# A conv-gated FFN on one core: from eight products of quarters in one pass to seven, in two passes through DRAM

## Chip, core and metric

The kernel runs on one core of one Trainium2 chip. The metric is the device time of one execution in microseconds; of several runs the median counts. All data are float32.

## What is computed

One decoder layer of width 1024 on 1024 tokens: four mixers side by side with an output projection, cross attention over 256 memory tokens, and an FFN with a causal depthwise convolution of width 3 ahead of a SiLU gate; a norm ends it. The FFN:

```python
D_MODEL, SEQ, BATCH, DEPTH, MEM_LEN, D_FF, FFN_CONV = 1024, 1024, 1, 1, 256, 2816, 3
...
def _conv_ffn(h, w_up, conv_w, w_down):
    u = _causal_dwconv(jnp.matmul(h, w_up), conv_w)
    gate, val = jnp.split(u, 2, axis=-1)
    return jnp.matmul(jax.nn.silu(gate) * val, w_down)
...
    mem_n = _rmsnorm(mem, mem_norm_w)
    h = x
    for l in range(DEPTH):
        h = h + _hybrid_mixer(_rmsnorm(h, mix_norm_w[l]), positions, ...)
        h = h + _memory_cross_attn(_rmsnorm(h, xattn_norm_w[l]), mem_n, ...)
        h = h + _conv_ffn(_rmsnorm(h, ffn_norm_w[l]), ffn_up[l], ffn_conv_w[l], ffn_down[l])
    return _rmsnorm(h, final_norm_w)
```

## The kernel before

**Matmuls in three parts.** Every large product is made of float32r parts: an operand is split into a high part (ScalarE casts it, line 865) and a low part (VectorE subtracts the high part from the source, line 103 by way of `split`), and three matmuls form hi x hi, lo x hi and hi x lo (`mm3`, lines 900, 901 and 903). Line 103 is the helper `tt`, through which every tensor_tensor of VectorE and GpSimd goes, so groups are told apart by their tiles.

**Stages.** The mixers' last part runs into the output projection (`wout`), which ends at 728 us, queries and scores follow, then the second output projection (`wo`), whose products `evac` adds to the residual `t`, stores to `hT` in DRAM, scales by the norm's gain and splits into `hh` and `hl`. `Sums` collects the squares; `rstd` makes the norm's factor `rbc` from them for each half of the tokens.

**FFN.** `ffn` runs one loop over f = 0 to 21, 128 hidden columns each. `hidden(f)` calls `conv_tile` for the gate (tiles `ug`, `zg`) and the value (`uv`, `zv`): a weight tile of 128 columns over all 1024 inputs (one load of 512 KB, `raw`, split into `whi` and `wlo`) is multiplied with both halves of the tokens, 8 x 3 matmuls of 512 columns each; VectorE multiplies the result by `rbc` (tokens' norm), ScalarE and VectorE form the convolution (lines 1519 and 1521), ScalarE the SiLU, VectorE the gate product and its low part (`hidh`, `hidl`). Two f behind, `down_proj` multiplies two f of hidden columns with two row blocks of `ffn_down` (`wdh`, `wdl`; the last call has four) and adds each result into `out`, eight blocks of 128 tokens. The last call also squares, scales by the final gain (GpSimd, `wbc`), forms the norm's factor in small steps on VectorE (`ss`, lines 136 to 142), scales and stores.

**Order.** A scheduler places the instructions on each engine when the program is built; each engine then runs its own list in order and waits on semaphores. All DMAs are issued by SyncE, in order. Tiles come from pools with a fixed number of buffers; a new tile waits until the old one in its place has been read.

## Time and profile before

| | us |
|---|---|
| median of 3 runs (range) | 1688.33 (1683.96 to 1690.45) |
| profiled execution, its own time | 1686.75 |
| its span, first to last instruction | 1685.0 |
| of it from the first FFN matmul to the end | 744.6 |

The profile names a group of instructions by engine, line, operation and tiles (`ug<-hh,whi`: written from read), with its count, busy time and mean duration. TensorE's matmuls overlap in the pipeline, so a mean of 390 ns is longer than the distance between two of them. An idle time is put down to the instruction that ended it. Of a window the profile gives each engine's busy time in it and the granted clock of TensorE as a share of the full one.

### The profile page before, as it was taken

The page shows a single profiled execution, that of the slowest core. Times are in us where ns is not written, and L with a number is a line of the kernel's source. Part 1 is how long each engine was busy: PE and PEld are TensorE (multiplying, and loading weights), DVE is VectorE, ACT ScalarE, POOL GpSimd, SP SyncE. Part 2 cuts the span into 40 slices and gives each one's busy share as a digit, 9 for nine tenths or more (in the row PEclk, how much of TensorE's full clock was granted, in tenths as well). Part 3 has the DMA queues.
Part 4 walks back from the last instruction along what each step waited for, and adds up shares of the span by engine and source line. Part 5 has one row for each costly group of instructions (what it writes and reads, how often), then busy time and mean ns, then how long its engine had stood idle before and what let it go on. Part 6 is the DMA issues. An engine that isn't in the chain of part 4 may idle for free.

```text
span 1685.0 us, 26532 instructions
## 1 busy us (share of the span) xinstructions
PE 1635.3 (97%) x10501; PEld 1366.0 (81%) x10501; DVE 1033.4 (61%) x1702; ACT 624.6 (37%) x1212; POOL 279.5 (17%) x330
## 2 busy tenths in 40 slices
PE   6999998999999999999999999999999999999996
PEld 6887786888877897788888888888888888888885
DVE  6765596536676545654565466557557556565577
ACT  6543633233474234343454352313213213123133
POOL 3401214323326414210012100000000000000013
PEclk8999999999999999999999999999999999999998
DMA  8743447663384344652245432102102112111012
GB/s 278 227 153 111 131 125 169 171 177 120 105 245 136 107 139 139 189 171 76 82 125 175 147 124 63 55 21 76 50 26 75 44 32 63 38 51 63 26 43 95
DMA packets 238551, 187.17 MB, mean 111 GB/s; under 512 B 34284, under 2 KB 210779, under 8 KB 238427
## 3 DMA queue, kind: packets, MB, share of 16 engines
q1 hardware_dynamic: 238427, 185.47, 36.3%
q8 instruction: 83, 1.36, 0.3%
q14 instruction: 41, 0.34, 0.1%
HBM read 138.75 MB, written 46.68 MB: 110 GB/s over the span
## 4 chain that ended last, share of the span: by engine, by line
PE 78%; DVE 9%; DMA 5%; issue 2%; ACT 2%; SPq 1%; POOL 1%; ACTq 0%; DVEq 0%; POOLq 0%
PE ug L903 5%; PE ug L900 5%; PE ug L901 5%; PE uv L901 5%; PE uv L903 5%; PE uv L900 5%; PE dn L900 4%; PE dn L903 4%; PE dn L901 4%; DVE wlo L103 2%; PE q L900 2%; PE wo L903 2%; PE wo L900 2%; PE q L901 2%; PE wo L901 2%
## 5 line engine op out<-in xcount | busy, mean ns | idle before, releaser
L103 DVE TENSOR_TENSOR wlo<-raw,whi 128x1024 fp32r<-128x1024 f32 (+1 forms) x150 | 196.2, 1308 | 108.6 <-ACT whi L865 101.3
L865 ACT CAST whi<-raw 128x1024 fp32r<-128x1024 f32 (+1 forms) x150 | 157.6, 1051 | 191.2 <-PE q L901 39.2
L103 DVE TENSOR_TENSOR out<-dn,out 128x512 f32<-128x512 f32 x160 | 109.2, 688 | 66.0 <-PE dn L903 65.4
L903 PE MATMUL ug<-hh,wlo 128*128 128x512 f32 x352 | 137.7, 392 | 0.0
L901 PE MATMUL ug<-hl,whi 128*128 128x512 f32 x352 | 137.3, 390 | 0.0
L900 PE MATMUL ug<-hh,whi 128*128 128x512 f32 x352 | 137.2, 390 | 0.0
L901 PE MATMUL uv<-hl,whi 128*128 128x512 f32 x352 | 137.1, 390 | 0.0
L903 PE MATMUL uv<-hh,wlo 128*128 128x512 f32 x352 | 137.1, 389 | 0.0
L900 PE MATMUL uv<-hh,whi 128*128 128x512 f32 x352 | 137.0, 389 | 0.0
L901 PE MATMUL dn<-wdl,hidh 128*128 128x512 f32 x320 | 124.7, 390 | 0.0
L900 PE MATMUL dn<-wdh,hidh 128*128 128x512 f32 x320 | 124.7, 390 | 0.0
L903 PE MATMUL dn<-wdh,hidl 128*128 128x512 f32 x320 | 121.9, 390 | 0.0
L1519 ACT ACTIVATE ug<-zg,taps 128x512 f32<-128x512 f32 x44 | 31.7, 722 | 201.1 <-DVE zg L103 196.5
L103 DVE TENSOR_TENSOR zg<-ug,rbc 128x512 f32<-128x512 f32 x44 | 30.2, 689 | 87.9 <-PE ug L903 87.9
L900 PEld LDWEIGHTS ug<-hh,whi 128*128 128x128 f32 x352 | 66.1, 188 | 14.0 <-issue 0.2
L901 PEld LDWEIGHTS ug<-hl,whi 128*128 128x128 f32 x352 | 66.1, 188 | 14.0
L903 PEld LDWEIGHTS ug<-hh,wlo 128*128 128x128 f32 x352 | 66.1, 188 | 13.9 <-issue 0.2
L900 PEld LDWEIGHTS uv<-hh,whi 128*128 128x128 f32 x352 | 66.1, 188 | 13.7
L903 PEld LDWEIGHTS uv<-hh,wlo 128*128 128x128 f32 x352 | 66.1, 188 | 13.6
L901 PEld LDWEIGHTS uv<-hl,whi 128*128 128x128 f32 x352 | 66.1, 188 | 13.6
L1521 DVE SCALAR_TENSOR_TENSOR ug<-zg,taps,ug 128x512 f32<-128x512 f32 x88 | 65.7, 750 | 13.1 <-ACT ug L1519 10.5
L865 ACT CAST hidh<-ug 128x512 fp32r<-128x512 f32 x44 | 27.3, 621 | 124.8 <-DVE ug L103 124.8
(463 smaller groups left out, 4166.1 us busy)
## 6 DMA issues: line engine op xcount, KB each, us to landing
raw<-in_ffn_up SPq DMA_DIRECT2D x44, 512.0 KB
raw<-in_w_in SPq DMA_DIRECT2D x26, 512.0 KB
raw<-in_ffn_down SPq DMA_DIRECT2D x22, 512.0 KB
raw<-in_w_out SPq DMA_DIRECT2D x16, 512.0 KB
hT<-t SPq DMA_DIRECT2D x32, 256.0 KB
raw<-in_xattn_wq SPq DMA_DIRECT2D x16, 512.0 KB
raw<-vod SPq DMA_DIRECT2D x16, 512.0 KB
raw<-in_xattn_wk SPq DMA_DIRECT2D x8, 512.0 KB
```

The costliest lines, as they stand in the source:

```text
L103: e.tensor_tensor(out=out, in0=a, in1=b, op=op)
L865: nc.scalar.copy(hi, src)
L900: nc.tensor.matmul(o, lhsT=w.hi, rhs=x.hi, start=first, stop=False)
L901: nc.tensor.matmul(o, lhsT=w.hi, rhs=x.lo, start=False, stop=False)
L903: nc.tensor.matmul(o, lhsT=w.lo, rhs=x.hi, start=False, stop=last)
L1519: S_.mul(u, z[:, 2 + o:2 + o + 512], taps[:, 2, n:n + 1])
L1521: V.scalar_tensor_tensor(u, z[:, j + o:j + o + 512], taps[:, j, n:n + 1], u, op0=ALU.mult, op1=ALU.add)
```

## The change

The FFN becomes two passes. Both products are cut into quarters (two halves of the tokens or hidden columns, two halves of what is summed over), and each 2 x 2 product of quarters is formed of seven products by the Winograd form of Strassen's algorithm, with sums and differences of quarters ahead of it and sums of the products behind it.

- *Up pass* (`ffn_up`): the four result quarters are gate and value columns of f, by the two halves of the tokens. The activations are now normed before they are split: the first half's blocks `x` (`early`) are made while the second half of `wo` runs, and the five combined blocks `t1`, `t2`, `t3`, `n4`, `b22` by `rest` after it. Of the weights, GpSimd forms four sums per f (`s1` to `s4`), and seven operands of 128x512 are split (`ws`) in place of two of 128x1024. Two of the seven products per f need only `early` and run three f ahead (`lead`). VectorE adds the products up (`u2`, `u3`, `zv1`, `zv0`, `zg1`) from PSUM; the convolution stays. The gate's weights are loaded twice.
- *Between*: instead of being split and used at once, the gated hidden columns go to DRAM as the seven left operands of the down product (`hd`, three as they are and four sums by GpSimd for each pair of f, `left_sums`), and GpSimd forms four differences of quarters of `ffn_down` for each pair (`right_sums`, `dd`).
- *Down pass* (`ffn_down_`): seven products, each over 11 pairs of operands that are loaded and split (left by VectorE, right by GpSimd), into four PSUM banks; sums into `out` by VectorE and GpSimd. The norm of token blocks 4 to 7 is finished ahead of the last product.
- Constants of the mixers move to a pool that is closed after them; the tiles of the two passes lie where older pools were.

```diff
-        h = cross_attention(K, ap_, h1p, hp2, h, r, xattn_wq[0], kd, vod, hT, col("ffn"), rbc)
+        prep = cross_attention(K, ap_, h1p, hp2, h, r, xattn_wq[0], kd, vod, hT, col("ffn"))
+        att2.close()
+        wts2.close()
+        down_ops = ffn_up(K, ap_, h1p, prep, ffn_up_w[0], ffn_conv_w, ffn_down[0])
         att.close()
-        ffn(K, ctx, h, rbc, ffn_up[0], ffn_conv_w, ffn_down[0], hT[1], final_norm_w, out)
+        hps.close()
+        ffn_down_(K, down_ops, ffn_down[0], hT[1], final_norm_w, out)
...
+        if hf == 0:
+            for k in range(NK):
...
+                t = wide(ap_, "x0")
+                nc.sync.dma_start(out=t, in_=hT[1][k][:, cs])
+                V.scalar_tensor_tensor(t, t, gain[:, k:k + 1], rb, op0=ALU.mult, op1=ALU.mult)
+                nc.sync.dma_start(out=xd[k], in_=t)
+                d = early[-1][:, k % 4]
+                split(K, t, d.hi, d.lo)
+    def rest(blocks):
+        t1, t2, t3, n4, b22 = blocks
...
+        for k in range(4):
+            x0 = wide(ap_, "x0")
+            nc.sync.dma_start(out=x0, in_=xd[k])
+            lo, hi = late[k], late[4 + k]
+            for j, t in ((k, lo), (4 + k, hi)):
+                V.scalar_tensor_tensor(t, t, gain[:, j:j + 1], rb, op0=ALU.mult, op1=ALU.mult)
+            tt(V, x0, lo, x0, ALU.subtract)
+            split(K, x0, t1[:, k].hi, t1[:, k].lo)
+            tt(V, x0, hi, x0, ALU.subtract)
+            split(K, x0, t2[:, k].hi, t2[:, k].lo)
...
+def product(K, acc, w, x, begin):
+    for k in range(4):
...
+        K.nc.tensor.matmul(acc, lhsT=a.hi, rhs=b.hi, start=begin and k == 0, stop=False, **o)
+        K.nc.tensor.matmul(acc, lhsT=a.hi, rhs=b.lo, start=False, stop=False, **o)
+        K.nc.tensor.matmul(acc, lhsT=a.lo, rhs=b.hi, start=False, stop=k == 3, **o)
+LEAD = 3
...
+                  {"raw": 3, "ws": 7, "s": 2, "dc": 4})
...
+        def lead(f):
+            g = columns(f)
+            acc = mx(K, "p12")
+            product(K, acc, parts(g[:, 0:4]), early[0], True)
+            u = wide(ap_, "u2")
+            S_.copy(u, acc)
+            product(K, acc, parts(g[:, 4:8]), early[1], False)
...
+            S_.copy(z[:, 2:], acc)
+            return u, z
...
+        def hidden(f, u2, zg0):
+            g, v = columns(f), columns(22 + f)
+            ws = {}
+            def total(name, a, b, op):
+                t = wp.tile([P, 4, P], F32, tag="s", name=name)
+                tt(G, t, a, b, op)
+                ws[name] = parts(t)
+                return t
+            s1 = total("s1", v[:, 0:4], v[:, 4:8], ALU.add)
+            s2 = total("s2", s1, g[:, 0:4], ALU.subtract)
+            acc = mx(K, "p6")
+            product(K, acc, ws["s2"], t2, True)
+            tt(V, u2, u2, acc, ALU.add)
+            total("s3", g[:, 0:4], v[:, 0:4], ALU.subtract)
...
+            product(K, c, ws["s3"], t3, True)
+            tt(V, u3, u2, c, ALU.add)
...
+            product(K, d, ws["s1"], t1, True)
+            tt(V, zv1[:, 2:], u3, d, ALU.add)
+            total("s4", g[:, 4:8], s2, ALU.subtract)
+            product(K, c, parts(v[:, 4:8]), n4, False)
+            tt(V, zv0[:, 2:], u2, c, ALU.add)
+            product(K, d, ws["s4"], b22, False)
+            tt(V, zg1[:, 2:], u2, d, ALU.add)
...
+            for zg, zv in ((zg0, zv0), (zg1, zv1)):
+                a, b = conv(zg, f, "ug"), conv(zv, 22 + f, "uv")
+                S_.activation(a, a, AF.Silu)
+                tt(V, a, a, b, ALU.mult)
...
+        def left_sums(j, e, o):
...
+            out(0, e[0]), out(1, o[0]), out(3, o[1])
+            total(6, e[0], e[1], ALU.subtract)
+            s1 = total(4, e[1], o[1], ALU.add)
+            s2 = total(5, s1, e[0], ALU.subtract)
+            total(2, o[0], s2, ALU.subtract)
+        def right_sums(j):
...
+            for i, (d, a, b) in enumerate(((b11, b12, b11), (b12, b22, b12), (b22, b22, b11), (b21, b21, b22))):
+                tt(G, d, a, b, ALU.subtract)
+                nc.sync.dma_start(out=dd[(0, 2, 1, 3)[i]][j], in_=d)
+        ahead = [lead(f) for f in range(LEAD)]
...
+        rest((t1, t2, t3, n4, b22))
+        for f in range(22):
+            res = hidden(f, *ahead.pop(0))
+            if f + LEAD < 22:
+                ahead.append(lead(f + LEAD))
...
+def ffn_down_(K, ops, down, hT, final_w, out):
...
+                  {"u": 8, "rh": 4, "hs": 13, "rd": 4, "ds": 13, "res": 2, "ss": 3})
...
+        def operand(src, raw, tag, eng):
+            r = bp.tile([P, 512], F32, tag=raw, name=raw)
+            nc.sync.dma_start(out=r, in_=src)
+            t = bp.tile([P, 2, 512], F32R, tag=tag, name=tag)
+            S_.copy(t[:, 0], r)
+            tt(eng, t[:, 1], r, t[:, 0].bitcast(F32), ALU.subtract)
...
+        def prod(i, accs, begin):
+            for j in range(11):
+                h, d = operand(hd[i][j], "rh", "hs", V), operand(right(i, j), "rd", "ds", G)
+                for a, ts in zip(accs, tiles):
+                    add(a, h, d, ts, begin and j == 0, j == 10)
```

What the scheduler makes of it, at three places. VectorE, one f in the middle of the loop before (`hidden` with its two weight tiles and a split of `ffn_down`):

```order
L103 TENSOR_TENSOR zg_13699<-ug_13707,rbc0_63 128x512
L1521 SCALAR_TENSOR_TENSOR ug_13733<-zg_13699,taps_9710,ug_13733 128x512 x2
L103 TENSOR_TENSOR zg_13699<-ug_13737,rbc1_64 128x512
L103 TENSOR_TENSOR wlo_13852<-raw_13849,whi_13851 128x1024
L1521 SCALAR_TENSOR_TENSOR ug_13763<-zg_13699,taps_9710,ug_13763 128x512 x2
L103 TENSOR_TENSOR zv_13767<-uv_13775,rbc0_63 128x512
L103 TENSOR_TENSOR wdl_13998<-raw_13995,wdh_13997 128x1024
```

VectorE now, a stretch of the 22 operations of one f (`ws` the low parts of weights, `u2<-u2,p6` and `u3<-u2,p74` sums that read PSUM):

```order
L1612 SCALAR_TENSOR_TENSOR ug_11991<-zg0_11519,taps_9736,ug_11991 128x512
L101 TENSOR_TENSOR ws_12189<-raw_12186,ws_12189 128x512
L1612 SCALAR_TENSOR_TENSOR uv_11995<-zv0_11950,taps_9736,uv_11995 128x512
L1612 SCALAR_TENSOR_TENSOR ug_12001<-zg1_11952,taps_9736,ug_12001 128x512
L101 TENSOR_TENSOR u2_11678<-u2_11678,p6_12078 128x512
L1612 SCALAR_TENSOR_TENSOR uv_12005<-zv1_11951,taps_9736,uv_12005 128x512
L101 TENSOR_TENSOR ws_12206<-raw_12186,ws_12206 128x512
L101 TENSOR_TENSOR ug_11991<-ug_11991,uv_11995 128x512
L1612 SCALAR_TENSOR_TENSOR ug_12001<-zg1_11952,taps_9736,ug_12001 128x512
L101 TENSOR_TENSOR u3_12110<-u2_11678,p74_12097 128x512
```

Splits of half the width and sums from PSUM now stand among the conv steps. GpSimd before, from the last sum of squares ahead of the FFN into the loop:

```order
L103 TENSOR_TENSOR acc1_9411<-acc1_9411,sq_9690 128x512
L1512 MEMSET zg_9851 128x2
L1512 MEMSET zv_9919 128x2
L1512 MEMSET zg_9999 128x2
L1512 MEMSET zv_10067 128x2
```

GpSimd now, in the up pass (`ls` left sums, `rs` right sums):

```order
L101 TENSOR_TENSOR ls_11710<-ug_11640,ls_11707 128x512
L101 TENSOR_TENSOR rs_11873<-rs_11875,rs_11873 128x512
L1604 MEMSET zg0_11870 128x2
L101 TENSOR_TENSOR rs_11875<-rs_11877,rs_11875 128x512
L101 TENSOR_TENSOR rs_11877<-rs_11877,rs_11873 128x512
L101 TENSOR_TENSOR rs_11879<-rs_11879,rs_11877 128x512
L101 TENSOR_TENSOR s1_12068<-raw_12066 128x512
L101 TENSOR_TENSOR s2_12073<-s1_12068,raw_12064 128x512
L1638 MEMSET zv0_11950 128x2
L101 TENSOR_TENSOR s3_12092<-raw_12064,raw_12066 128x512
L101 TENSOR_TENSOR ls_12052<-ug_11815,ug_11825 128x512
L101 TENSOR_TENSOR s4_12130<-raw_12064,s2_12073 128x512
```

The additions are new on this engine; weight sums stand between left sums, which read VectorE's results. SyncE before, where `ffn_down` is first loaded (a load stands among others and has its own buffer):

```order
L1542 DMA raw_10443<-in_ffn_down 128x1024
L1503 DMA res_9835<-hT1_7338 128x512
L1503 DMA res_9843<-hT1_7338 128x512
L1542 DMA raw_10449<-in_ffn_down 128x1024
L892 DMA raw_10593<-in_ffn_up 128x8x128
```

SyncE now, at the turn from the up to the down pass:

```order
L1660 DMA hd3_9751<-ug_13680 128x512
L1660 DMA hd4_9752<-ls_13696 128x512
L1660 DMA hd5_9753<-ls_13699 128x512
L1660 DMA hd2_9750<-ls_13702 128x512
L1714 DMA wbc_13717<-in_final_norm_w 128x1024
L1722 DMA rh_13723<-hd0_9748 128x512
L1722 DMA rd_13728<-in_ffn_down 128x512
L1722 DMA rh_13745<-hd0_9748 128x512
```

The down pass's loads (`rh`, `rd`) stand behind the last stores of left sums.

## Rows read from the trace of the kernel before

**Rows 1.** The page's busy table: busy us, share of the span, instructions.
```profile
span 1685.0 us, 26532 instructions
...
PE 1635.3 (97%) x10501; PEld 1366.0 (81%) x10501; DVE 1033.4 (61%) x1702; ACT 624.6 (37%) x1212; POOL 279.5 (17%) x330
```

**Rows 2.** Windows by stage: us, busy by engine (instructions), PEclk, DMA share, GB/s.
```profile
940.00:1030.00 90.00, 90.00 (x428) 74.23 (x427) 53.27 (x72) 42.64 (x61) 2.99 (x11) 1.00 0.37 120
1030.00:1130.00 100.00, 100.00 (x442) 82.65 (x441) 59.53 (x82) 20.19 (x28) 0.50 (x5) 1.00 0.13 41
1630.00:1685.00 55.00, 39.60 (x171) 31.71 (x169) 40.89 (x129) 16.98 (x41) 20.62 (x16) 0.91 0.21 77
```

**Rows 3.** Tile `ug` (ns min/median/max, first and last start); the timeline's last matmul.
```profile
L900 PE MATMUL ug<-hh,whi x352: 387/389/510, 940.4 to 1613.3; 128*128 128x512 f32 x176
...
1669.20 0.40 PE L903 MATMUL dn<-whi,hidl 128*128 128x512 f32 x1
```

**Rows 4.** Timeline of VectorE where it has a queue: start, us, operation.
```profile
980.10 0.68 DVE L103 TENSOR_TENSOR ug<-ug,uv 128x512 f32<-128x512 f32 x1
980.70 0.74 DVE L1521 SCALAR_TENSOR_TENSOR ug<-zg,taps,ug 128x512 f32<-128x512 f32 x1
981.37 0.68 DVE L103 TENSOR_TENSOR hidl<-ug,hidh 128x512 fp32r<-128x512 f32 x1
981.97 1.41 DVE L1521 SCALAR_TENSOR_TENSOR ug<-zg,taps,ug 128x512 f32<-128x512 f32 x2
```

**Rows 5.** Groups by line: count, busy us, mean ns, idle before.
```profile
L103 POOL TENSOR_TENSOR out<-out,wbc 128x512 f32<-128x512 f32 x16 | 20.6, 1294 | 49.8 <-ACT sq L1565 49.8
...
L865 ACT CAST hidh<-ug 128x512 fp32r<-128x512 f32 x44 | 27.3, 621 | 124.8 <-DVE ug L103 124.8
```

**Rows 6.** Timelines of VectorE and GpSimd where both work at once.
```profile
1649.40 0.16 DVE L141 SCALAR_TENSOR_TENSOR ss<-ss 128x1 f32<-128x1 f32 x1
1649.42 1.30 POOL L103 TENSOR_TENSOR out<-out,wbc 128x512 f32<-128x512 f32 x1 [1.71 <-ACT sq L1565]
1649.60 1.15 DVE L142 SCALAR_TENSOR_TENSOR ss<-ss 128x1 f32<-128x1 f32 x1
...
614.39 0.68 DVE L103 TENSOR_TENSOR xl<-ot,xh 128x512 fp32r<-128x512 f32 x1
614.60 1.04 POOL L103 TENSOR_TENSOR oev<-oev,rs 128x512 f32<-128x512 f32 x1 [4.68 <-DVE zev L103]
615.00 1.20 DVE L103 TENSOR_TENSOR zev<-zev,oev 128x512 f32<-128x512 f32 x1
...
863.45 0.75 DVE L869 SCALAR_TENSOR_TENSOR hl<-t,cols,hh 128x512 fp32r<-128x512 f32 x1
863.58 1.77 POOL L103 TENSOR_TENSOR acc<-acc,sq 128x512 f32<-128x512 f32 x1 [5.88 <-ACT sq L1084]
```

**Rows 7.** Timeline: the second half's norm, first activation and last operation.
```profile
951.45 0.69 ACT L129 ACTIVATE rbc<-rps,consts 128x512 f32<-128x512 f32 x1 [5.55 <-PE rps L124]
...
957.13 0.69 DVE L103 TENSOR_TENSOR rbc<-rbc,nt 128x512 f32<-128x512 f32 x1
```

**Rows 8.** Timeline: a load of 256 KB is issued, and the operation that waits for it.
```profile
923.28 0.43 SPq L1473 DMA_DIRECT2D t<-hT  x1
...
927.34 0.69 DVE L103 TENSOR_TENSOR t<-wo,t 128x512 f32<-128x512 f32 x1 [0.65 <-DMA t<-hT]
```

**Rows 9.** Windows near the start, columns as in rows 2.
```profile
12.00:16.00 4.00, 1.54 (x5) 1.25 (x6) 4.00 (x7) 1.93 (x3) 1.52 (x1) 0.58 1.01 401
...
20.00:24.00 4.00, 4.00 (x37) 4.00 (x36) 2.98 (x7) 4.00 (x8) 2.62 (x2) 1.00 0.89 274
```

**Rows 10.** Timeline of the tail: the last row block's addition.
```profile
1676.16 0.68 DVE L103 TENSOR_TENSOR out<-dn,out 128x512 f32<-128x512 f32 x1
```

## What the change is expected to do

> **What bounds the kernel now.** I read the busy table first: TensorE is busy for 97% of the span, VectorE for 61%, GpSimd for 17% [rows 1]. That invites the thought that fewer matmuls mean less time. The table by stage then says where: from 940.4 us, where the first matmul of the FFN starts [rows 3], to the end, 744.6 of 1685.0 us are FFN. In its middle TensorE never stops, at full granted clock: 442 matmuls in 100.00 us, one each 0.226 us, while VectorE works 59.5 us of 100 and GpSimd 0.5 [rows 2]. There TensorE sets the pace, and the other two have room. At the very end it is otherwise: the last matmul starts at 1669.20 [rows 3], the last row block is added at 1676.16 [rows 10], and VectorE is busy 40.9 us of the last 55 [rows 2].
>
> **What is removed.** Up is 44 x 2 x 8 x 3 = 2112 matmuls of 512 columns before, down 22 x 8 x 2 x 3 = 1056. Seven products in place of eight give 22 x 7 x 12 = 1848 and 7 x 11 x 4 x 3 = 924. That is 396 fewer, at 0.226 us: **-89.6 us**, if TensorE still sets the pace. One step of 128 hidden columns (one f) costs TensorE 96 x 0.226 = 21.7 us before and 84 x 0.226 = 19.0 us after. Everything else is a question of whether the others keep up with 19.0.
>
> **What is added in the up pass.** The order of VectorE and GpSimd shows the pattern. Per f VectorE has 22 operations of 128x512: seven splits of weights, five sums that read one operand from PSUM, eight conv steps, two gate products. Where VectorE has a queue in the trace, a tensor_tensor follows the next after 0.60 us and a conv step after 0.67 [rows 4], so it needs 14 x 0.60 + 8 x 0.67 = 13.8 us. Alone that fits under 19.0. ScalarE has seven casts of about 0.62 [rows 5] and seven copies and activations, under 10 us, and is not late. GpSimd, which had only memsets here, gets eight additions per f: four sums of weights, and four for the operands of the down pass (right sums on even f, left sums on odd). A GpSimd operation of this shape and with two inputs takes 1.29 us [rows 5]: 10.4 us per f.
>
> These two cannot be put side by side. In the tail of the trace a VectorE operation on one column takes 0.16 us, and 1.15 when a GpSimd multiply has just started; at 614.60 a GpSimd operation of 1.04 us lets the operation that reads PSUM pass at its usual 0.68, and the next, with both inputs in SBUF, takes 1.20 in place of 0.68. At 863.58 it is GpSimd that waits: its addition lasts 1.77, until 1.15 us after VectorE's step has ended [rows 6]. So an addition on GpSimd and an operation of VectorE with two SBUF inputs take turns. The Trainium skill has this as a rule, in "SBUF — State Buffer", section "Who interferes with whom": a VectorE instruction with two SBUF inputs contends with a GpSimd instruction that reads SBUF, and whoever is second waits for the whole of the other; with one SBUF input it does not contend. Taken literally, with the row's 1.29 held whole, an addition would cost 0.22 us more than below, 1.8 us per f, and the sum would be some 38 us higher; the rows show the shorter hold, and I go by them.
>
> Of the 22 operations 17 have two SBUF inputs and five read PSUM. An addition that comes before one of the 17 costs VectorE about 1.05 us (0.16 to 1.15, and the waits of the others alike); before one of the five some 0.5, since that one passes meanwhile. Mean: (17 x 1.05 + 5 x 0.5) / 22 = 0.93, times eight = 7.4 us. VectorE then needs 13.8 + 7.4 = 21.2 us per f, and I add 0.2 for a place where it waits for GpSimd itself (a weight sum stands behind a left sum in GpSimd's queue): **21.4 us per f, which is above TensorE's 19.0**. Bounds: below, TensorE's own 19.0 (all additions fall into waits of VectorE); above, 13.8 + 10.4, all of GpSimd's time added, 24.2. I take 21.4 because in a full queue the additions have no waits to fall into. So VectorE sets the pace of the up pass.
>
> **The path, step by step.** (1) Second half of the output projection: between two of its weight splits VectorE gets ten operations, 6 us, where a weight tile lasts 24 x 0.226 = 5.4; TensorE waits some 2 us: the projection ends at 942.4. (2) The first weights of the up pass lie where the old weight pool lies, and their loads stand behind it. A load of half the size lands 4.06 us after its issue [rows 8]; six casts follow, then the last norm: from its first activation at 951.45 to its last operation at 957.13, 0.69 long, the trace has 6.4 us [rows 7]. VectorE starts on the activations' operands at about 956.4, 14 us later. Meanwhile TensorE waits some 6 us and then has six lead products, 16.5 us. (3) The five combined blocks: 41 operations of VectorE, 25 us, and 16 of GpSimd's additions among them, 16 x 0.93 = 15: 996. (4) From there to the end of the up pass VectorE has 473 operations in its order, 21.5 times 22: 21.5 x 21.4 = 460: 1456. (5) The turn to the down pass: in SyncE's order the first loads of the down pass stand behind the last store of the up pass, and that behind GpSimd's last left sum. Three sums of 1.29, four issues of about 0.4, a landing of 3.5, two casts, one split of 1.29: 11 us in which TensorE has nothing. After its first long wait the trace granted it 0.58 of the clock on average in 12 to 16 us, much of that at the lower of its two levels (1.2 and 2.4 GHz), and the full clock from 20 [rows 9]; the same here costs about 3 us more: 1470. (6) Down pass: 924 x 0.226 = 209, and 12 for the transposes of the residual and what lay between the matmuls of the FFN before (1669.6 - 940.4 - 3168 x 0.226): 1691. A pair of operands costs VectorE 0.6 and GpSimd 1.29 against TensorE's 12 x 0.226 = 2.7, with 13 buffers ahead: hidden; GpSimd's 28 other operations, 36 us, fit too (77 x 1.29 + 36 = 135 of 209). If they did not, up to 15 us would come on top. (7) Tail: one addition and one multiply per row block are left where there were two each; from the last block's addition to the end it is 8.8 us [rows 1, 10], and I take 12 from the last matmul on, where 15.4 were: 1703 to 1704.
>
> The span of the profiled execution is 1685.0, its time 1686.75, so 1.75 lies around it; the median of the runs shown is 1.6 us above that time. **1704 + 1.75, about 1706 us**, 1.0% slower than the median. The 90 us that TensorE is spared are spent by VectorE (21.4 - 19.0 over 21.5 steps, 52 us), by the start (some 25), and by the turn between the passes (some 30 with the last conv).
>
> **Rivals.** A, faster: GpSimd's additions fall into gaps in which VectorE waits for ScalarE or TensorE anyway. For it speaks that VectorE's order was laid out with such waits; against it that a queue of 13.8 us of work with eight interruptions leaves few. If all are hidden, TensorE sets the pace: from 949, 22 x 19.0 = 418 and a wait of 10 for the first blocks, 17 for the last conv and the turn, 3, 221, 12, 1.75: 1632. It decides from where a step falls below 21.4 - (1706 - 1688)/21.5 = 20.5 us: there the kernel is no longer slower. Half hidden is about 1660. B, slower still: the queues lock step. Three weight buffers per f, GpSimd's and SyncE's queues in fixed order, and a load of the next weights that stands behind a store of a left sum: one wait of a sum, a cast and a split, 2.6 us per f, gives 24 us and 1762. For it speaks that these queues mix work of both kinds; against it that a load has some 12 us of VectorE's order to land in. That the change does not do what it says is no rival: the order has the fewer matmuls.
>
> **How the numbers follow.** The forecast (a step between 20.3 and 22.8 us) has 0.55, with 1680 to 1737 as its own range; A 0.27, with 1632 to 1680; B 0.18, with 1737 to 1790. A tenth is left out on either side: 1645 to 1758. 0.5%, about 8.4 us, is what a measurement of this kernel can tell from no change: below 1680 lies A with 0.26; 1680 to 1697 takes 0.17, the lower part of the forecast; above it 0.57.
>
> **What would show it.** Right: a step of the up pass of 21 to 22 us, TensorE idle some 2 us in each, its waits put down to VectorE's or ScalarE's split of weights; VectorE's splits and conv steps at a mean well above 0.69 and 0.75 while the sums that read PSUM stay at 0.69; a gap of TensorE of 15 to 20 us before the down pass, and a down pass without gaps. Wrong: TensorE above 97% busy in the up pass (A), or VectorE idle for several us of each step, waiting for GpSimd or a load (B).

## The result: 1.2% slower, with the parts at other sizes

The changed kernel took a median of 1706.46 us (1703.65 to 1708.32), the kernel before, run beside it, 1686.14 (1681.43 to 1690.45): a ratio of 1.012, 95% interval 1.0085 to 1.0155. The profiled execution took 1704.68, of which the span is 1702.5. Of the four runs of `v1_right_early`, in the table further down, one took 2548.85 us at a granted clock of 0.555 where the others have 0.973 to 0.980, and the time given there is the median of these three. The busy table, against [rows 1]:

```profile
span 1702.5 us, 27454 instructions
...
PE 1579.4 (93%) x10105; PEld 1301.4 (76%) x10105; DVE 1149.9 (68%) x1745; ACT 736.4 (43%) x1514; POOL 694.1 (41%) x605
```

TensorE has 396 fewer matmuls and is busy 56 us less, but the span is 17.5 us longer. Where it idles stands in the windows by stage (columns as in [rows 2]):

```profile
943.00:960.00 17.00, 15.91 (x57) 11.71 (x58) 12.54 (x14) 10.00 (x15) 8.80 (x8) 0.81 0.80 249
960.00:995.00 35.00, 20.30 (x61) 13.45 (x59) 31.16 (x33) 14.70 (x27) 20.53 (x15) 0.76 0.39 120
...
1100.00:1400.00 300.00, 282.31 (x1172) 224.46 (x1171) 268.55 (x308) 122.27 (x236) 170.60 (x141) 0.97 0.51 165
...
1450.00:1470.00 20.00, 4.35 (x10) 3.47 (x11) 8.48 (x11) 5.91 (x10) 7.97 (x6) 0.50 0.69 249
```

In [rows 2] TensorE was busy 100.00 of 100 us in the middle of the FFN; here it is 282.31 of 300, VectorE is at 268.55 where it had 59.5 of 100, and GpSimd at 170.60. TensorE's large holes are the start of the FFN and the turn between the passes. Its timeline (start, duration, idle time before it in brackets) has them, a small one in the down pass, and the last matmul:

```profile
944.09 2.07 PE L129 MATMUL rps<-acc,ones 128*128 128x512 f32 x2 [10.59 <-POOL acc L101]
...
1465.65 2.07 PE L1730 MATMUL dn<-ds,hs 128*128 128x512 f32 x4 [21.91 <-ACT ds L1724]
...
1503.03 2.08 PE L1730 MATMUL dn<-ds,hs 128*128 128x512 f32 x4 [3.52 <-ACT ds L1724]
...
1693.36 0.39 PE L1732 MATMUL dn<-ds,hs 128*128 128x512 f32 x1
```

The length of a step of the up pass is read from one small operation that each step has once, ScalarE's copy of two columns into `zv`; these are the copies of f = 3 and f = 19:

```profile
1072.21 0.19 ACT L1642 COPY zv<-zv 128x2 f32<-128x2 f32 x1
...
1418.02 0.19 ACT L1642 COPY zv<-zv 128x2 f32<-128x2 f32 x1
```

Sixteen steps in 345.81 us are **21.6 us each**; VectorE is busy 268.55/300 of that, 19.3 us, and idles 2.3. All steps below are read in this way.

How GpSimd and VectorE meet is seen in the timeline of VectorE, and under it GpSimd's of the same moment:

```profile
1056.79 0.74 DVE L1612 SCALAR_TENSOR_TENSOR uv<-zv,taps,uv 128x512 f32<-128x512 f32 x1
1057.46 1.78 DVE L101 TENSOR_TENSOR ws<-raw,ws 128x512 fp32r<-128x512 f32 x1
1059.16 1.78 DVE L101 TENSOR_TENSOR ug<-ug,uv 128x512 f32<-128x512 f32 x1
1060.86 0.67 DVE L101 TENSOR_TENSOR u<-u,p 128x512 f32<-128x512 f32 x1
...
1057.07 3.32 POOL L101 TENSOR_TENSOR rs<-rs 128x512 f32<-128x512 f32 x2 [0.74 <-POOL rs L101]
1060.35 1.72 POOL L101 TENSOR_TENSOR s<-raw 128x512 f32<-128x512 f32 x1
```

Two operations of VectorE with both inputs in SBUF last 1.78 in place of 0.68, the next, which reads PSUM (`p`), its usual 0.67; GpSimd's own last 1.7 in place of 1.29. Over the stretch from 1100 to 1400 us the groups by line (count, busy us, mean ns, idle time before) say the same: splits, conv steps and gate products at about 1.0 us, sums from PSUM at 0.675.

```profile
L101 DVE TENSOR_TENSOR ws<-s,ws 128x512 fp32r<-128x512 f32 x56 | 59.9, 1078 | 30.2 <-ACT ws L870 30.2
L1612 DVE SCALAR_TENSOR_TENSOR uv<-zv,taps,uv 128x512 f32<-128x512 f32 x56 | 55.3, 987 | 0.0
...
L101 DVE TENSOR_TENSOR ug<-ug,uv 128x512 f32<-128x512 f32 x28 | 31.9, 1139 | 0.7
L101 DVE TENSOR_TENSOR zv<-u,p 128x512 f32<-128x512 f32 x28 | 18.9, 675 | 0.5 <-PE p L1554 0.5
```

These means mix operations that were held with operations that were not: of the conv steps `uv` the median has 743 ns and the longest 1781. The waits of the same stretch (us in total, times, longest) form a chain. TensorE waits for VectorE's sums, VectorE for ScalarE's casts of weight sums, and ScalarE for GpSimd, which makes these sums:

```profile
ACT ws L870 <- POOL s L101: 104.0, 27, 9.6
...
DVE ws L101 <- ACT ws L870: 30.2, 15, 3.1
...
PE p L1552 <- DVE u L101: 16.1, 6, 3.5
```

### The profile page after: what moved, and what is told of

Same layout as the page of the kernel before. It is cut to its first block, busy times and chain, and to the rows that moved or that the text cites. A ratio compares the mean times of both kernels' runs of the same rounds, so it can differ in the third digit from the quotient of the medians.

```text
span 1702.5 us, 27454 instructions
## 1 busy us (share of the span) xinstructions
PE 1579.4 (93%) x10105; PEld 1301.4 (76%) x10105; DVE 1149.9 (68%) x1745; ACT 736.4 (43%) x1514; POOL 694.1 (41%) x605
## 3 DMA queue, kind: packets, MB, share of 16 engines
q1 hardware_dynamic: 307531, 275.34, 51.6%
q8 instruction: 79, 1.29, 0.3%
## 5 line engine op out<-in xcount | busy, mean ns | idle before, releaser
L101 DVE TENSOR_TENSOR wlo<-raw,whi 128x1024 fp32r<-128x1024 f32 (+2 forms) x104 | 133.5, 1283 | 87.0 <-ACT whi L870 80.4
L870 ACT CAST whi<-raw 128x1024 fp32r<-128x1024 f32 (+2 forms) x104 | 109.1, 1050 | 155.2 <-PE q L906 42.0
L101 DVE TENSOR_TENSOR hs<-rh,hs 128x512 fp32r<-128x512 f32 x77 | 92.5, 1222 | 99.4 <-ACT hs L1724 97.1
L1730 PE MATMUL dn<-ds,hs 128*128 128x512 f32 x308 | 115.9, 399 | 25.4 <-ACT ds L1724 25.4
L101 POOL TENSOR_TENSOR ds<-rd,ds 128x512 fp32r<-128x512 f32 x77 | 114.6, 1507 | 57.8 <-ACT ds L1724 56.7
L1731 PE MATMUL dn<-ds,hs 128*128 128x512 f32 x308 | 122.2, 397 | 0.0
L1732 PE MATMUL dn<-ds,hs 128*128 128x512 f32 x308 | 121.5, 394 | 0.0
L101 DVE TENSOR_TENSOR ws<-s,ws 128x512 fp32r<-128x512 f32 x88 | 89.5, 1028 | 45.2 <-ACT ws L870 45.1
L1553 PE MATMUL p<-t,ws 128*128 128x512 f32 x264 | 107.6, 407 | 4.8 <-DVE t L101 4.7
L1552 PE MATMUL p<-t,ws 128*128 128x512 f32 x264 | 107.0, 407 | 5.2 <-ACT ws L870 2.9
L1554 PE MATMUL p<-t,ws 128*128 128x512 f32 x264 | 107.0, 407 | 3.3 <-DVE ws L101 3.3
L101 POOL TENSOR_TENSOR rs<-rs 128x512 f32<-128x512 f32 x44 | 71.2, 1618 | 48.4 <-DMA rs<-in_ffn_down 25.8
L1730 PEld LDWEIGHTS dn<-ds,hs 128*128 128x128 f32 x308 | 58.7, 193 | 38.1 <-ACT ds L1724 26.1
L1612 DVE SCALAR_TENSOR_TENSOR uv<-zv,taps,uv 128x512 f32<-128x512 f32 x88 | 87.4, 997 | 0.0
L1552 PE MATMUL p<-x,ws 128*128 128x512 f32 x176 | 69.4, 404 | 8.0 <-ACT u L1601 8.0
L1553 PE MATMUL p<-x,ws 128*128 128x512 f32 x176 | 70.5, 401 | 0.0
L1554 PE MATMUL p<-x,ws 128*128 128x512 f32 x176 | 70.4, 401 | 0.0
```

The costliest lines, as they stand in the source:

```text
L101: e.tensor_tensor(out=out, in0=a, in1=b, op=op)
L870: nc.scalar.copy(hi, src)
L1552: K.nc.tensor.matmul(acc, lhsT=a.hi, rhs=b.hi, start=begin and k == 0, stop=False, **o)
L1553: K.nc.tensor.matmul(acc, lhsT=a.hi, rhs=b.lo, start=False, stop=False, **o)
L1554: K.nc.tensor.matmul(acc, lhsT=a.lo, rhs=b.hi, start=False, stop=k == 3, **o)
L1612: V.scalar_tensor_tensor(u, z[:, j:j + 512], taps[:, j, n:n + 1], u, op0=ALU.mult, op1=ALU.add)
```

## The experiments

Two theories. *Turns*: GpSimd's additions and VectorE's operations with two SBUF inputs take turns, and this sets the step. *Queue*: the step is set by a loop through GpSimd's and SyncE's queues (buffer free, load, sum, cast, split). All kernels were timed beside the kernel before; the ratios are to it. The order of each engine's list is laid out anew for every kernel, so an edit also moves some instructions: compared by operation and tile in the traces, of VectorE's 1745 operations in the changed kernel 1725 keep their order in `e10_stores_gpsimd`, some 1690 in `e1_no_sums` and `e6_more_s`, 1620 in `e8_no_turns`, 1600 in `e5_conv_psum` and 1590 in `e9_psum_and_s`.

| kernel | us | ratio (95% interval) | step, us | VectorE busy in it |
|---|---|---|---|---|
| the change | 1706.46 | 1.012 (1.0085 to 1.0155) | 21.6 | 19.3 |
| e1_no_sums | 1657.1 | 0.9823 (0.9804 to 0.9842) | 19.6 | 14.4 |
| e2_all_vector | 1679.86 | 0.9955 (0.9938 to 0.9971) | 20.0 | 18.9 |
| e3_weights_vector | 1694.82 | 1.0032 (1.0018 to 1.0046) | 20.8 | 19.8 |
| e4_leftright_vector | 1694.36 | 1.0050 (1.0034 to 1.0067) | 20.7 | 19.6 |
| v1_right_early | 1675.95 | 0.9922 (0.9897 to 0.9948) | 19.4 | 17.6 |
| e5_conv_psum | 1719.43 | 1.0176 (1.0151 to 1.0201) | 21.7 | 16.0 |
| e6_more_s | 1701.38 | 1.0063 (1.0038 to 1.0089) | 20.8 | 20.6 |
| e8_no_turns | 1655.84 | 0.9798 (0.9782 to 0.9814) | 19.3 | 14.2 |
| e9_psum_and_s | 1740.02 | 1.0284 (1.0263 to 1.0305) | 22.4 | 17.5 |
| v2_right_in_q | 1675.22 | 0.9919 (0.9893 to 0.9945) | 19.4 | 17.6 |
| e10_stores_gpsimd | 1723.86 | 1.0200 (1.0183 to 1.0217) | 22.3 | 20.5 |

**What all additions cost.**

```diff
-                t = wp.tile([P, 4, P], F32, tag="s", name=name)
-                tt(G, t, a, b, op)
+                t = a
...
-                t = wp.tile([P, 512], F32, tag="dc", name="ls")
-                tt(G, t, a, b, op)
+                t = a
...
-                tt(G, d, a, b, ALU.subtract)
```

The three places are the weight sums, the left sums and the right sums.

> Left out: all eight additions of GpSimd in each step of the up pass; a weight sum or an operand of the down pass is then simply its first summand, with the same splits, products and stores, so TensorE's work is that of the changed kernel. In the changed kernel a step of the up pass lasts 21.6 us (two steps 43.0) where its 84 matmuls at 0.226 us are 19.0. Theory (GpSimd's additions and VectorE's operations with two SBUF inputs take turns, and that sets the step): VectorE needs 13.8 us of a step, TensorE sets the pace again, the step falls to 19.0 to 19.5, and the time by 21 x 2.3 = 48, to about 1657; splits and conv steps fall from a mean of 1.0 to 0.69 and 0.75. Rival (what limits is the distance from a weight's load to its split, or the loads and stores themselves, which stay): under a third of that, 1690 or more. The turn to the down pass (21.9 us of TensorE) shrinks by the three last sums, 4 us, under both.

1657.1, as expected. TensorE is busy without a break, and a step is the 19.6 us of its 84 matmuls, 0.233 each:

```profile
1100.00:1400.00 300.00, 300.00 (x1291) 242.59 (x1289) 220.12 (x341) 135.37 (x259) 2.81 (x28) 1.00 0.38 120
```

So the additions on GpSimd cost the kernel 49 us. It takes away turns and queue alike; the next ones tell these apart.

**The same additions on VectorE**, all or half of them (`tt(G` to `tt(V` in the lines above).

> All eight additions of a step are on VectorE, none on GpSimd. Theory (turns between GpSimd and VectorE set the step): VectorE then needs 13.8 + 8 x 0.60 = 18.6 us, less than the 21.2 that it needs with the turns, though it does more; TensorE's 19.0 sets the pace, with some waits since the two are so near: 19.0 to 20.3 a step, 1652 to 1680. Rival (VectorE is late because it has too much in its queue, not because of GpSimd): 18.6 + the 2.2 us a step that VectorE waits now = 20.8 or more, 1690 and above.

> The four sums of weights of a step are on VectorE, the four for the down pass stay on GpSimd. Theory (turns, 0.93 us of VectorE for each addition on GpSimd): 13.8 + 4 x 0.60 + 4 x 0.93 = 19.9, a step of 20.1, 1.5 x 21.5 = 32 us less: about 1674. Rival (not the turns but the way of a weight sum through GpSimd's queue, a cast and a split makes TensorE wait): all that can be had is had here, 19.2 a step, about 1655, and nothing in the kernel with the other four moved.

> The four additions of a step for the operands of the down pass are on VectorE, the four sums of weights stay on GpSimd. Theory (turns): the same as with the weights moved, 13.8 + 2.4 + 3.7 = 19.9 for VectorE, about 1674. Rival (the way of a weight sum through GpSimd's queue is what counts): the weight sums have the same way as before, less the places where they stand behind a left or right sum: 0 to 10 us less, 1696 to 1706.

With eight more operations in its list VectorE is busy 18.9 us a step, less than the 19.3 that it had without them, and the kernel is 26 us faster: that speaks for turns, and the time lies at the upper end of what was expected.

```profile
1100.00:1400.00 300.00, 290.44 (x1247) 233.35 (x1245) 282.51 (x453) 135.62 (x255) 2.88 (x29) 1.00 0.55 175
```

But of the 1.6 us that a step lost, only some 0.5 is VectorE's busy time. The other 1.1 is time in which it idled: 2.3 us of a step in the changed kernel, 1.1 here. So GpSimd's additions cost VectorE waits as well as busy time.

Four of eight moved give 12 us, whichever four, where 32 were expected, and VectorE's busy time even grows by 0.3 to 0.5, so all of this gain is in the waits. With the left and right sums moved the 12 us are nearer to the rival's 0 to 10 than to the theory. That it doesn't matter which four speaks against the queue of the weight sums as the sole cause; that it is 12 says that the price of 0.93 was too high.

**The price by itself**, in the kernel before, where nobody waits for the result.

```diff
     def hidden(f):
+        for _ in range(8):
+            tt(G, spare, wbc[:, 0:512], wbc[:, 512:1024], ALU.add)
```

> The kernel before, with eight additions of 128x512 on GpSimd added for each f, two inputs in SBUF, for whose result nobody waits: the price of one addition by itself. VectorE is busy 19.7 of the 33.1 us of an f there (up and down together). Theory (turns): VectorE's busy time in the FFN grows by 0.6 to 0.93 for each addition, 5 to 7.4 us per f, its splits and conv steps grow, its operations that read PSUM do not, and as 27 us is still under 33.1 TensorE and the time stay as they are, 1680 to 1695. Rival (what made the changed kernel's VectorE slow was something else, as its own operands or the loads): VectorE's busy time as before, within 0.5 us per f.

The additions did not spread; they ran in bunches of up to 22, and the last of the 176 ended at 1262 us. In the window 1030 to 1130 GpSimd is busy 92.88 us, and VectorE needs 79.84 for 68 operations where [rows 2] has 59.53 for 82:

```profile
1030.00:1130.00 100.00, 90.69 (x384) 73.57 (x383) 79.84 (x68) 23.83 (x33) 92.88 (x65) 0.95 0.15 43
```

The groups from 1030 to 1530 us have conv steps at 1.16 and leave the products that read PSUM (`zg<-ug,rbc`) untouched; the kernel before has 750 and 690 ns there. More than half of that stretch has no additions: from 1030 to 1130 alone the conv steps `ug` are at 1.68.

```profile
L1521 DVE SCALAR_TENSOR_TENSOR ug<-zg,taps,ug 128x512 f32<-128x512 f32 x56 | 64.8, 1156 | 8.0 <-ACT ug L1519 5.5 <-POOL spare L103 0.9
...
L103 DVE TENSOR_TENSOR zg<-ug,rbc 128x512 f32<-128x512 f32 x28 | 19.3, 689 | 50.8 <-PE ug L903 50.8
```

The kind of effect is as expected, the price is lower. Over the whole FFN VectorE is busy 547.05 us, and 463.13 in the kernel before: 83.9 us for 176 additions, 0.48 each, where 0.6 to 0.93 were expected. First the kernel with the additions, then the kernel before:

```profile
940.00:1739.00 799.00, 742.99 (x3244) 608.69 (x3243) 547.05 (x698) 210.46 (x305) 300.41 (x238) 0.97 0.18 55
```

```profile
940.00:1685.00 745.00, 729.60 (x3240) 601.88 (x3238) 463.13 (x697) 211.99 (x304) 27.13 (x62) 0.99 0.18 58
```

The time was a miss: 50 us more (1740.36 beside 1690.35) in place of none, since in a bunch VectorE does fall behind TensorE, which waited 27.0 us for `zv`. A share of VectorE over a whole f hides that.

**Turns without queue, queue without turns.** First one more buffer for the weight sums (`"s": 2` to `"s": 3`), then the conv's running sums in PSUM:

```diff
-            u = wide(ap_, name)
-            S_.mul(u, z[:, 2:514], taps[:, 2, n:n + 1])
-            for j in (1, 0):
-                V.scalar_tensor_tensor(u, z[:, j:j + 512], taps[:, j, n:n + 1], u, op0=ALU.mult, op1=ALU.add)
+            u, ps = wide(ap_, name), mx(K, "cv")
+            S_.mul(ps, z[:, 2:514], taps[:, 2, n:n + 1])
+            for d, j in ((ps, 1), (u, 0)):
+                V.scalar_tensor_tensor(d, z[:, j:j + 512], taps[:, j, n:n + 1], ps, op0=ALU.mult, op1=ALU.add)
```

> One change of a number: three buffers in place of two for the sums of weights, so that GpSimd waits less often for VectorE to have split the last one. In the changed kernel VectorE idles 2.3 us of a step of 21.6. Theory (turns): the busy 19.3 us stay, of the 2.3 up to half goes, 0 to 1.1 us a step, 1682 to 1706. Rival (the queues lock step through the few buffers): 1.5 us a step or more, 1673 or less.

> The running sums of the conv lie in PSUM until their last step writes them to SBUF, so that the eight conv steps per step of the up pass read one operand from SBUF and one from PSUM; nothing else changes, all eight additions stay on GpSimd. VectorE's busy time per step is 19.3 us in the changed kernel and 14.4 without GpSimd's additions, so these cost 4.9 us of it. Theory (only an operation with two SBUF inputs takes turns with GpSimd): 8 of 17 such operations are out of it, 4.9 x 8/17 = 2.3 us less, a step of 19.6 to 20.3, 1666 to 1682; conv steps at 0.74 throughout, splits still above 0.9. Rival (GpSimd slows whatever VectorE does, or the step comes from the wait for the weight sums): conv steps still near 1.0, 1700 or more. Not told apart by it: if the four shared PSUM buffers make TensorE wait for the conv, that shows as waits of TensorE for VectorE's conv.

With the third buffer the step is 20.8, and VectorE is busy 296.43 of 300 us: there it has no waits left, and its busy time with the turns in it is the limit. The 0.8 us that the step lost are put down to the queue with two buffers, as little else moved. They are less than the 2.3 us that VectorE idled, since its busy time rose from 19.3 to 20.6 when the waits went. The kernel's time fell by 5 us only (the profiled executions by 8.6), not least because the steps began later: the copy of f = 3 stands at 1075.73, not at 1072.21.

```profile
1100.00:1400.00 300.00, 286.42 (x1215) 228.37 (x1213) 296.43 (x316) 127.15 (x245) 193.35 (x150) 0.99 0.56 174
```

With the conv in PSUM its steps are at 0.74 to 0.75, as the theory of turns has it. Of the splits those of weight sums stay long, 0.99 where they had 1.08, but those of loaded weights fell to 0.78. And the time, 1719.43, is in the rival's range, not the theory's: the step did not shorten. What VectorE saved, 3.3 us, came back as waits, for ScalarE's casts (51.6 us where the changed kernel has 30.2) and for TensorE (15.0 at `zv` where it has 0.5). ScalarE itself now waited 46.9 us for weight buffers that TensorE held, 5.7 in the changed kernel. So this run neither shows nor refutes that the turns set the step: another limit took their place. The four PSUM buffers, shared by more tiles, are the likely one, but no run tests it.

```profile
L101 DVE TENSOR_TENSOR ws<-s,ws 128x512 fp32r<-128x512 f32 x56 | 55.4, 989 | 51.6 <-ACT ws L870 51.2
...
L1612 DVE SCALAR_TENSOR_TENSOR cv<-zv,taps,cv 128x512 f32<-128x512 f32 x28 | 21.0, 751 | 6.9 <-ACT cv L1610 6.4
...
L101 DVE TENSOR_TENSOR zv<-u,p 128x512 f32<-128x512 f32 x28 | 19.3, 689 | 15.0 <-PE p L1554 14.5
```

**The test that settles it.** An addition is replaced by one of two columns and two memsets, which occupy GpSimd and read nothing:

```diff
+def fill(G, t, a, b, op):
+    tt(G, t[:, 0:2], a[:, 0:2], b[:, 0:2], op)
+    for _ in range(2):
+        G.memset(t[:, 2:512], 0.0)
...
-                tt(G, t, a, b, op)
+                fill(G, t, a, b, op)
```

> Each of GpSimd's eight additions of a step becomes an addition of two columns and two memsets of the rest, which read nothing: the same tiles, the same waits and the same place in GpSimd's queue, about 1.2 us each, but hardly any reading of SBUF. The sums' values are left out by it. With the conv's running sums in PSUM VectorE was busy only 16.0 us of a step, and the step stayed at 21.7, so the turns cannot be all. Theory A (turns alone set the step): 19.6 to 19.9 us a step, as with no additions at all, 1657 to 1666. Theory B (the loop through GpSimd's queue alone: buffer free, sum, cast, split): 21.3 or more, 1698 to 1706. Theory C (both: VectorE's busy time with the turns is one limit, near 20.8, and the loop, whose parts the turns lengthen, is the other): 19.9 to 21.2, 1666 to 1696.

1655.84, as with no additions at all and just under the range of theory A. The window, VectorE's tiles (min/median/max ns) and one of GpSimd's groups:

```profile
1100.00:1400.00 300.00, 297.37 (x1283) 240.49 (x1281) 220.15 (x344) 137.15 (x260) 164.37 (x399) 1.00 0.56 177
```

```profile
L101 DVE TENSOR_TENSOR ws<-s,ws x60: 677/684/694, 1108.2 to 1381.8; 128x512 fp32r<-128x512 f32 x60
...
L1618 DVE SCALAR_TENSOR_TENSOR uv<-zv,taps,uv x65: 737/744/750, 1100.6 to 1399.1; 128x512 f32<-128x512 f32 x65
```

```profile
L1405 POOL MEMSET s<- 128x510 f32 x118 | 59.5, 521 | 0.4
```

GpSimd is busy 10.6 us a step, as eight additions of 1.29 alone would make it (12.3 in the changed kernel, where VectorE holds up the additions too), yet no operation of VectorE is held: the longest split has 694 ns, the longest conv step 753. And the queue is no better off; GpSimd's waits in the same stretch (us in total, times, longest), first here, then in the changed kernel:

```profile
POOL s L101 <- DMA raw<-in_ffn_up: 63.7, 13, 8.3
...
POOL s L101 <- DVE ws L101: 41.5, 20, 6.6
```

```profile
POOL s L101 <- DVE ws L101: 40.0, 21, 3.2
POOL s L101 <- DMA raw<-in_ffn_up: 39.9, 7, 6.7
```

The waits are there, and cost nothing as long as the parts of the loop are not lengthened. Of the three ranges only A's fits: without the reading, TensorE sets the pace. So GpSimd's reading beside VectorE is the cause of the long step. The run takes the holding off both engines at once; it does not tell how much of the lost time is VectorE's own longer operations and how much is GpSimd's sums coming later. For that there is only the third buffer's 0.8 us and the change in idle time above. The Trainium skill says in "SBUF — State Buffer", section "Who interferes with whom", that a VectorE instruction with two SBUF inputs contends with a GpSimd instruction that reads SBUF, and not with one that only writes; the trace agrees, splits of 694 ns at most beside memsets and of 1.78 us beside additions.

**Two that failed.**

> Two single edits together: the conv's running sums in PSUM, which alone left the step at 21.7 (VectorE busy 16.0 of it), and three buffers for the weight sums, which alone gave 20.8 (VectorE busy 20.6 of it). Theory C (two limits that lie close together): with both loosened 19.6 to 20.6 a step, 1668 to 1692, less than either alone. Theory B, or PSUM buffers that make TensorE wait: 20.8 or more, 1697 and above.

> The four stores of left sums in every second step are issued from GpSimd's queue, each right behind its own addition, so that no load of weights stands behind one in SyncE's queue any longer (SyncE waited 67.7 us of 300 for left sums there). Rival B of the prediction (a load behind a store closes the loop): 0.5 to 1.5 us a step less, 1672 to 1695. Theory that the loop runs through the weight sums' own buffers instead: within 0.3 us a step, 1699 to 1712.

The two edits together gave 22.4 us a step, worse than either: not theory C's range, but the one expected of theory B or of waits for PSUM buffers. TensorE waits 25.6 us of 300 for the sum `u`, and ScalarE 99.8 for weight buffers that TensorE holds. Four PSUM buffers serve the conv, the first products and the early ones in these two kernels, and the lists' order differs most here; which of the two lengthens the step stays open. Moving the stores gave a step of 22.3 and 1723.86 us, outside both ranges, though VectorE's list is almost the same. GpSimd's waits for loads of weights fell (26.1 us of 300 where the changed kernel has 39.9), but those for right sums' loads grew from 10.7 to 32.5, and GpSimd now issues the stores itself, 0.56 us each:

```profile
L1660 POOL DMA_DIRECT2D hd<-ls x25 | 13.9, 557 | 3.9 <-POOL ls L101 3.9
```

So a load behind a store, as rival B had it, is not shown to cost anything here; what lengthened the step stays open.

**A version that beats both.** The right sums need only weights, so they can be made where VectorE has room; weight and left sums go to VectorE. The first lines of the diff stand behind the weight tiles of `wout` and act at every fourth, with the like for the queries and `wo`; the second version drops them for `wout` and has two groups in place of one for each four tiles of the queries.

```diff
+                if k % 4 == 2:
+                    next(K.right, None)
...
-                tt(G, t, a, b, op)
+                tt(V, t, a, b, op)
...
-                right_sums(f // 2)
```

> The 44 right sums (differences of the down weights, which need nothing of the activations) are taken out of the up pass and made on GpSimd between 620 and 930 us, one group of four at every fourth weight tile of the three projections there; the sums of weights and the left sums are on VectorE, so GpSimd adds nothing in the up pass. VectorE then has 28 operations a step; with eight fewer it was busy 14.4 us a step, 0.65 each, so 18.3 where TensorE's 84 matmuls took 19.6 with nothing in their way. Theory (turns with GpSimd made VectorE late, and one queue that is full adds waits of its own): TensorE sets the pace, 19.6 to 19.9 a step, 1657 to 1668, against 1680 with all eight on VectorE and 1688 of the kernel before. Rival (the additions cost as much where they are put, since VectorE has two-input operations there too, and the extra 23 MB of transfers stand in the way of weight loads): 10 us and more later at the end of the output projection, 1675 or above.

> As the version with the right sums made early, but eight of the eleven groups in the projection of the queries and three in the first half of the output projection, none in the mixers' output projection, which lasted 108.6 us in place of 94.5 with them, at a DMA share of 0.91. The step of the up pass stays at 19.4. If the loads alone were what slowed that stage, 10 to 14 us come back less up to 4 for the queries: 1664 to 1672. If the additions cost VectorE and TensorE as much there, 1675 to 1680.

The first took 1675.95 us, ratio 0.9922 (0.9897 to 0.9948). The step is 19.4 with TensorE busy 300.00 of 300:

```profile
1100.00:1400.00 300.00, 300.00 (x1294) 242.78 (x1293) 272.19 (x432) 140.79 (x263) 2.90 (x29) 1.00 0.40 125
```

From the start of the last matmul of `wo` to the end of the span it is 718.7 us, where the kernel before has 744.9, the change 769.4 and the kernel with no turns 716.3. The rest of the gain was lost ahead of the FFN, where the rival held: the output projection `wout` lasted 108.6 us (94.6 in the changed kernel), and the DMA share from 640 to 780 us is 0.91 (0.53). The second was to move the work out of that stretch and did not: the lists' layout pulled it forward, and in both versions all 44 additions ran between 654 and 800 us. So it tells nothing of the cause. The windows 640 to 780 of the two:

```profile
640.00:780.00 140.00, 129.01 (x560) 102.84 (x560) 79.09 (x96) 50.88 (x70) 86.76 (x58) 0.99 0.91 289
```

```profile
640.00:780.00 140.00, 129.49 (x563) 103.40 (x563) 80.95 (x97) 50.95 (x72) 89.29 (x61) 0.99 0.89 284
```

## Why the prediction was right, step by step

The time of 1706.0 met 1706.46, and the mechanism named as the cause is shown to be one: without GpSimd's reading the step is TensorE's. But of the terms several were off, and they cancelled; that the sum came within 1 us is luck.

- **TensorE's 19.0 us per f**: 19.3 to 19.6 where nothing stands in its way. In the up pass a matmul takes 0.232 us (300.00/1291 in `e1_no_sums`, 300.00/1294 in `v1_right_early`), not the 0.226 of [rows 2].
- **VectorE's 21.4 us per f**: 21.6, but made up otherwise. Without turns VectorE is busy 14.4 (said: 13.8). An addition costs it (19.3 - 14.4)/8 = 0.62, not 0.93, and 0.78 with the third buffer, where its list is always full. The mis-sized term is the price, which assumed that every addition meets a full list and holds the next operation: more than half of the conv steps `uv` were not held at all. Where these additions fell, beside a PSUM operation, in a wait or behind VectorE, was not counted. The 0.2 us for waits measured 2.3, of which the third buffer gives back 0.8 net. So VectorE does not set the pace alone, as was said: it idles a tenth of each step, and the turns' smaller price and the larger wait add up to the same step.
- **(1)** The projection was to end at 942.4; its last matmul starts at 933.1. That is no gain of the change: with the same instructions ahead, the experiments' traces have 934.6 to 942.5, and the kernel before 940.1. The profiled execution had some 5 us of luck there.
- **(2), (3)** TensorE's wait was 10.6 us, not 6; VectorE starts on the operands at 957.70 (956.4), and the blocks are split by 1003, 70 us after the projection where 54 were said: 24 to VectorE's start (14) and 46 for the blocks (40). In the 35 us from 960 on TensorE is busy 20.3. So this term was 16 us too small, and the luck of (1) hid half of it.
- **(4)** VectorE's last gate product ends at 1454.4 (1456), though it began later: the last three steps have no early products left to make, and the last two take 15.0 and 10.6 us.
- **(5)** From there to the first matmul of the down pass it is 11.2 us (11). TensorE's gap is 21.9 (15 to 20), as its list ends 10 us ahead of VectorE's conv. The clock: granted 0.50 in the gap, 0.85 from 1470 to 1475 and 1.00 after; ten matmuls in the 4 us from 1466 and 20 in the next 5 are some 10 fewer than at full clock, 2.2 us (3):

```profile
1466.00:1470.00 4.00, 4.00 (x10) 3.12 (x10) 3.45 (x3) 3.39 (x6) 3.86 (x3) 0.50 1.06 395
1470.00:1475.00 5.00, 5.00 (x20) 4.00 (x19) 4.08 (x4) 3.63 (x6) 4.48 (x4) 0.85 1.05 386
1475.00:1480.00 5.00, 5.00 (x24) 4.14 (x23) 5.00 (x4) 4.41 (x8) 5.00 (x4) 1.00 0.93 312
```

- **(6)** From first to last matmul 228 us (221): one wait of 3.5 us, that at 1503, behind the residual's transposes.
- **(7)** 8.7 us from the end of the last matmul (12).
- **Rivals.** A was what no turns would give, and was put at 1632; measured, it is 1656 to 1657, as TensorE's floor, the start and the down pass are each longer than said. B's wait for a sum, a cast and a split is there as 30.2 us of 300, 2.2 of a step; removing one cause of it, the few buffers, gave 0.8. That a load behind a store makes it, as B had it, was not confirmed. The third reading, the Trainium skill's rule with the whole of an addition held each time, gave 38 us more; the longest holds are 1.1 us (1.78 - 0.68), near the whole, but the mean is half of it.

What would have shown it was named rightly: splits and conv steps at 1.0, PSUM sums at 0.68, the gap before the down pass. TensorE's idle time is 1.3 us of a step (17.69 of 300), not 2, and its waits are put down to VectorE's sums `u`, not to the splits.

## What to carry to other kernels

When work goes to an idle GpSimd, count it on VectorE's time as well, if both read SBUF with two-input operations: here 0.5 to 0.8 us for each addition of 1.29, about as much as the 0.6 that VectorE needs to do the addition itself, and waits come on top. Where VectorE is as full as here, such work is better put on VectorE itself, or into a stage where VectorE waits anyway. And a sum that comes out right is no proof of its terms: only taking the suspect away, with the waits and the queue kept, showed what it costs.

## What was not expected of the hardware

- The distance between matmuls of 512 columns differs with the stage at a granted clock of 1.00: 0.227 us in the FFN of the kernel before and in the down pass, 0.232 to 0.233 in the up pass and 0.230 to 0.232 in `wo`, up to 3% more. What sets it was not tried.
- GpSimd suffers as well: its sums `s<-raw` have a mean of 1.56 us in the changed kernel (1.29 in [rows 5], which the prediction used for all eight).
- A store issued from GpSimd's queue in place of SyncE's took 0.56 us of GpSimd (`e10_stores_gpsimd`, 25 stores).
